# Forming a layer's new h in the block of the projection that it adds, with other steps for the sums behind it

## The chip, the cores and the metric

The kernel runs on one core of one Trainium2 chip. The metric is the device time of one execution in microseconds (us), the median over runs. The engines are named as the profile names them: PE is TensorE (matmuls; PEld its weight loads), ACT is ScalarE, DVE is VectorE, POOL is GpSimd, SP is SyncE, which here issues most transfers.

## The reference, cut to what matters

Two layers over a sequence of 512 positions with 2048 channels. Layer 0 is an attention and recurrent block, layer 1 a gated block with mixing along the sequence. After each, a gate product adds a projection of a second input:

```python
for i in range(2):
    xn = rms_norm(h, norm_pre[i])
    ...                                     # layer 0: y from attention and recurrence
    proj = xn @ c_w_in[j]                   # layer 1: 2048 x 6144
    u, v, g = _split(proj, (2048, 2048, 2048))
    oc = chunked_spatial_gating(u, v, ...)  # u * (tril(w_s) @ layer_norm(gelu(v)) + b_s), 16 groups
    y = (oc * jax.nn.silu(g)) @ c_w_out[j]
    h = h + rms_norm(y, norm_post[i])
    h = h + (p[i] @ ple_w_proj[i]) * jax.nn.sigmoid(h @ ple_w_gate[i])
```

The diff lies in three places: the last line of layer 0 (the gate product), the scaling by `norm_pre[1]` that opens layer 1, and the mixing in `chunked_spatial_gating`.

## The kernel before, in words

All operands are float32, split in a high and a low part, so that a product needs three matmuls: high by high, low by high, high by low. A big product is made by `seven`, a scheme of seven products in place of eight over blocks of the operands. Sums and differences of blocks are its operands; `sums` makes them (`x2`, `s1`, `s24`, `s3`, `x22`), and `put` and `finish` write each as a high part (a cast on ACT, L973) and a low part (a subtraction on DVE, L974) into its place. Places are slots with names: `yl0` to `yl15`, `xl0` to `xl15`, `yh0` to `yh15`, `xh0` to `xh3`; with `SETS`, the operand of `x2` goes into yl0 to yl7 and that of `s24` into xl0 to xl15.

Each product walks over its weights in eight pieces, a pair of column blocks over 14 products in 112 pieces. Each piece is cast on ACT (`whi`, L1544) and its low part made on DVE (`wlo`, L1545); every fifth piece goes to a place of its own, `half0` and `half1`. Four places for `whi` and `wlo` and one for `half` let the two engines be five pieces ahead of PE. At every piece `tick` counts one up and runs the side steps that are due; `later(n, step)` puts a step n pieces ahead. A scheduler then places each instruction in its engine's queue by priority and its own costs; each engine works its queue in order.

`first_gate` makes layer 0's gate product. The projection's blocks `pj[q, e]` come back from DRAM (`qd`, L1115) into slots whose old operands are no longer needed: (4,0), (5,0), (0,0), (1,0) into `xh0`; (2,0), (3,0) into yl0, yl1; (2,1), (3,1), (0,1), (1,1) into yl2 to yl5; (6,0), (7,0) into yl6, yl7; (6,1), (7,1), (4,1), (5,1) into xl0 to xl3. When a block of the product is done, `emit` runs: sigmoid on ACT (L1155), times `pj` on DVE (L1156), added to `H[q, e]` in its place (L1157), squared on ACT (L1159), squares summed on DVE (L1161). A save of 256 KB, `hd<-yh`, is issued on SP (L1163; every H block has a yh slot). Sixteen pieces later `scaled` multiplies H in its place by `norm_pre` on ACT, in two halves (L1169, 32 in all). It writes what the save reads, so it waits until that save has landed. `issue_after` keeps it behind the weight cast of its piece.

The sums of layer 1 take the scaled H: `early` and `x2` during the last pieces of the gate product, the others as steps in the first pieces of the next stage. In `layer_c` (values V, then U and G) the function `mix` does one of 16 groups of the mixing: it loads values and weights, normalizes (L1668 on ACT), splits into high and low part (L1678 to L1684) and multiplies with three matmuls (L1689 to L1691), at −11, −4, 0 and 5 pieces around its place.

Of the kernel before, what the change touches and what calls it, by code (L numbers as in the profile page):

```python
# [11 lines left out]
AF = mybir.ActivationFunctionType  # L12
ALU = mybir.AluOpType
# [56 lines left out]
def f(ap):  # L70
    return ap.bitcast(F32)
# [35 lines left out]
class Net:  # L107
# [986 lines left out]
    def first_gate(self, H, state, wp, ps):  # L1094
        nc, tc, i = self.nc, self.tc, self.i
        s, update, s1, s24, s3, x22 = state
        npre = self.cols["norm_pre"]
        accq, seen, pj, last = [], [False, False], {}, {}

        def places():  # L1100
            accq.extend((self.t(wp, [P, T], "accq", bufs=1), self.rstdB))

        def late(q):
            update(q, 1)
            update(q + 4, 1)
            s1(q)

        def first(q):
            with tc.high_priority(150):
                s24(q)  # L1110

        def fetch(tiles, *which):
            for (q, e), tl in zip(which, tiles):
                pj[q, e] = tl.rearrange("p (a t) -> p a t", a=2)
                nc.sync.dma_start(pj[q, e], self.qd[:, 2 * q : 2 * q + 2, e * 256 : e * 256 + 256])  # L1115

        def first_fetch():
            tl = self.t(self.xp, [P, 4, T], "xh0")
            fetch([tl[:, k, :] for k in range(4)], (4, 0), (5, 0), (0, 0), (1, 0))

        def next_fetch(n, *which):
            fetch([self.slot("yl", n + k, F32) for k in range(len(which))], *which)

        def x4():
            s[4] = self.place(("xh", (0, 3)))

        def x7():
            s[7] = self.place(("xh", (1, 2)))

        C = self.sums(H, wp, SETS)  # L1130
        cs, x2 = C[0], C[2]

        def early(q):
            if q == 0:
                cs[1] = self.whole_set()
            self.put(cs[1], q, H[q, 0])

        steps = [((1, 6, 19, 28)[q], lambda q=q: late(q)) for q in range(4)]
        steps += [((11, 15, 32, 35)[q], lambda q=q: first(q)) for q in range(4)]
        steps += [((23, 26, 43, 45)[q], lambda q=q: s3(q)) for q in range(4)]  # L1140
        steps += [(17, first_fetch), (22, places), (21, x7)]
        steps += [(34, lambda: next_fetch(0, (2, 0), (3, 0))), (44, lambda: next_fetch(2, (2, 1), (3, 1), (0, 1), (1, 1)))]
        steps += [(49, x4)]
        steps += [(50 + q, lambda q=q: x22(q)) for q in range(4)]
        steps += [(76, lambda: next_fetch(6, (6, 0), (7, 0)))]
        steps += [(90, lambda: fetch([self.slot("xl", k, F32) for k in range(4)], (6, 1), (7, 1), (4, 1), (5, 1)))]
        steps += [(103 + q, lambda q=q: early(q)) for q in range(4)]
        steps += [(110 + 2 * q, lambda q=q: x2(q)) for q in range(4)]
        for n, step in sorted(steps, key=lambda x: x[0]):
            self.later(n, step)  # L1150

        def emit(pr, m, n, src):
            e, q = m // 2, 2 * n + m % 2
            sv = src.rearrange("p (a t) -> p a t", a=2)
            last["act"] = nc.scalar.activation(src, src, AF.Sigmoid)  # L1155
            nc.vector.tensor_tensor(sv, sv, pj[q, e], ALU.mult)  # L1156
            nc.vector.tensor_tensor(H[q, e], H[q, e], sv, ALU.add)  # L1157
            sq = self.tmp(wp, "sq") if seen[e] else accq[e].rearrange("p (a t) -> p a t", a=2)
            nc.scalar.activation(sq, H[q, e], AF.Square)  # L1159
            if seen[e]:  # L1160
                nc.vector.tensor_tensor(accq[e], accq[e], sq.rearrange("p a t -> p (a t)"), ALU.add)  # L1161
            seen[e] = True
            nc.sync.dma_start(self.hd[:, 2 * q : 2 * q + 2, e * 256 : e * 256 + 256], H[q, e])  # L1163

            def scaled():
                for a in range(2):
                    c = 16 + 2 * q + a
                    with tc.issue_after(self.cast.ins):
                        nc.scalar.activation(H[q, e][:, a, :], H[q, e][:, a, :], AF.Copy, scale=npre[:, c : c + 1])  # L1169

            self.later(16, scaled)

        W = i["ple_w_gate"][0]
        self.seven(FIRST(*[Pair(W, 2 * j * T, 2 * j, emit) for j in range(2)]), Sets(s), ps, fm=True)
        s1, s24, s3, x22 = C[3:]
        steps = [(17 + 2 * q, lambda q=q: s1(q)) for q in range(4)]
        steps += [(25 + 3 * q, lambda q=q: s24(q)) for q in range(4)]
        steps += [(37 + 3 * q, lambda q=q: x22(q, True)) for q in range(4)]
        steps += [(48 + 3 * q, lambda q=q: s3(q)) for q in range(4)]
        return accq, last["act"], cs, steps  # L1180

# [434 lines left out]
    def layer_c(self, cp, sets, steps, accq, after, wp, ps):  # L1616
        nc, tc, i = self.nc, self.tc, self.i
# [29 lines left out]
        def mix(g, at):  # L1647


            gs = slice(g * P, (g + 1) * P)  # L1650
            fl = lambda x: x.rearrange("p m c -> p (m c)")
            own = {}

            def load():
                par = self.t(wp, [P, T], "accq", bufs=1) if g % 2 else self.rstdB
                own["ws"], own["bc"] = par[:, 0:P], par[:, P : 3 * P].rearrange("p (a c) -> p a c", c=P)
                vn = own["vn"] = self.t(wp, [P, 4, P], "sq")
                with tc.issue_after(self.cast.ins):
                    nc.scalar.dma_start(vn, self.vd[:, g])
                nc.scalar.dma_start(own["ws"], i["c_w_s"][0, g])  # L1660
                nc.scalar.dma_start(own["bc"][:, 0, :], i["c_ln_g"][0, gs].partition_broadcast(P))
                nc.scalar.dma_start(own["bc"][:, 1, :], i["c_ln_b"][0, gs].partition_broadcast(P))

            def norm():
                ws, bc, vn = own["ws"], own["bc"], own["vn"]
                row = lambda j: bc[:, j : j + 1, :].broadcast_to([P, 4, P])
                for m in range(4):
                    nc.scalar.activation(  # L1668
                        vn[:, m, :], vn[:, m, :], AF.Identity, bias=nb[:, m : m + 1], scale=rv[:, m : m + 1]
                    )  # L1670
                nc.gpsimd.affine_select(ws, ws, [[-1, P]], ALU.is_ge, 0.0, 0, 1)
                nc.vector.tensor_tensor(vn, vn, row(0), ALU.mult)
                nc.vector.tensor_tensor(vn, vn, row(1), ALU.add)

            def split():
                vn = own["vn"]
                pw = self.t(ps, [P, P], "mm")
                nc.tensor.transpose(pw, own["ws"], self.ident)  # L1678
                w2 = own["w2"] = self.t(lp, [P, 2, P], "w2", F32R)
                nc.scalar.copy(w2[:, 0], pw)  # L1680
                nc.vector.tensor_tensor(w2[:, 1], pw, f(w2[:, 0]), ALU.subtract)
                vh, vl = own["v"] = [self.t(wp, [P, 4, P], "sg", F32R) for _ in range(2)]
                nc.scalar.copy(vh, vn)
                nc.vector.tensor_tensor(vl, vn, f(vh), ALU.subtract)  # L1684

            def mul():
                w2, (vh, vl) = own["w2"], own["v"]
                pm = self.t(ps, [P, 4, P], "mm")
                nc.tensor.matmul(fl(pm), w2[:, 0], fl(vh), start=True, stop=False)  # L1689
                nc.tensor.matmul(fl(pm), w2[:, 0], fl(vl), start=False, stop=False)  # L1690
                nc.tensor.matmul(fl(pm), w2[:, 1], fl(vh), start=False, stop=True)  # L1691
                ub = u[g // 4][:, :, g % 4 * P : g % 4 * P + P]
                nc.vector.scalar_tensor_tensor(ub, pm, self.bsT[:, g : g + 1], ub, ALU.add, ALU.mult)

            for n, step in ((-11, load), (-4, norm), (0, split), (5, mul)):
                self.later(at + n, step)

        V = [Pair(W, D + 2 * j * T, 2 * j, vals) for j in range(2)]
# [36 lines left out]
        def done(step):  # L1735
# [28 lines left out]
            for j in range(2):  # L1764
                if step == nv + 14 * j + 1:
                    for e in range(8):
                        mix(8 * j + e, 40 + int(6.8 * e))
# [281 lines left out]
```

## Time and profile before

| | us |
|---|---|
| runs (3), median | 2232.8 |
| lowest, highest | 2230.08, 2234.23 |
| profiled execution | 2231.2 |
| its span | 2229.5 |
| PE busy | 2191.7 (98%) |
| DVE busy | 1660.8 (74%) |
| ACT busy | 1355.4 (61%) |

The span is the time that the profiler sees between the first and the last instruction; 1.7 us lie around it. Times of rows are us from the span's start. PE's busy time at the lower granted clock counts as busy, so its share does not show that loss; the column PEclk of the table by stretches does. The gate product of layer 0 fills 1230 to 1376, layer 1's product with c_w_in follows, with mixing from about 1610 to 1860.

### The profile page before, as it was taken

To read this page: it belongs to the slowest core of one execution; us is meant where nothing else is said; L and a number is where in the kernel's file an instruction comes from. 1 tells how busy PE (TensorE), PEld (TensorE's weight loads), DVE (VectorE), ACT (ScalarE), POOL (GpSimd) and SP (SyncE) were. 2 spreads that over 40 slices of the span, in tenths; PEclk is the share of its full clock that TensorE was granted. 3 is DMA by queue.
4 is the path that set the end of the run, shared out by engine and by line. 5 is a ranking of instruction groups with operands and counts; after the bars stand their busy time and mean duration, and the time that the engine had idled before them with its cause. 6 is when DMAs were issued, how large, how long until landed. Compare 5 with 4: busy or idle time off the path is not lost. (4 is left out here: it accounts for less than half of the span.)

```text
span 2229.5 us, 43456 instructions
## 1 busy us (share of the span) xinstructions
PE 2191.7 (98%) x16535; PEld 1876.3 (84%) x16535; DVE 1660.8 (74%) x3228; ACT 1355.4 (61%) x2764; POOL 311.6 (14%) x360
## 2 busy tenths in 40 slices
PE   9999999999999999999999999999999999999998
PEld 7878888888888788889999998787877878999887
DVE  8766667656734777886879877886677678978977
ACT  5545545555544677775667656755566567757754
POOL 2001010101000000000210121311121221120031
PEclk9999999999999999999999999999999999999999
DMA  7322322223233633327897887788779777688796
GB/s 237 93 78 62 84 77 79 72 64 89 69 99 95 207 103 101 97 84 208 169 226 231 201 204 190 178 211 222 167 160 231 170 187 185 146 192 271 208 242 169
DMA packets 304143, 343.34 MB, mean 154 GB/s; under 512 B 15757, under 2 KB 187950, under 8 KB 302910
## 3 DMA queue, kind: packets, MB, share of 16 engines
q1 hardware_dynamic: 237438, 240.93, 34.7%
q0 software_dynamic: 44608, 85.99, 22.5%
q10 hardware_dynamic: 21888, 13.64, 2.2%
q8 instruction: 130, 2.13, 0.4%
q14 instruction: 79, 0.65, 0.1%
HBM read 305.61 MB, written 34.90 MB: 153 GB/s over the span
## 5 line engine op out<-in xcount | busy, mean ns | idle before, releaser
L1545 DVE TENSOR_TENSOR wlo<-rq,whi 128x512 fp32r<-128x512 f32 x485 | 330.6, 688 | 138.4 <-ACT whi L1544 135.3
L1544 ACT CAST whi<-rq 128x512 fp32r<-128x512 f32 x485 | 298.4, 621 | 189.5 <-PE mm L1580 121.4
L213 PE MATMUL mm<-xh,whi 128*128 128x512 f32 x992 | 411.7, 415 | 0.0
L215 PE MATMUL mm<-xh,wlo 128*128 128x512 f32 x992 | 391.8, 395 | 0.0
L214 PE MATMUL mm<-xl,whi 128*128 128x512 f32 x992 | 389.6, 393 | 0.0
L197 ACT CAST whi<-raw 128x512 fp32r<-128x512 f32 x272 | 168.0, 619 | 149.9 <-PE mm L214 103.2
L199 DVE TENSOR_TENSOR wlo<-raw,whi 128x512 fp32r<-128x512 f32 x272 | 186.0, 695 | 92.6 <-ACT whi L197 70.0
L215 PEld LDWEIGHTS mm<-xh,wlo 128*128 128x128 f32 x992 | 186.2, 188 | 41.2
L213 PEld LDWEIGHTS mm<-xh,whi 128*128 128x128 f32 x992 | 186.9, 188 | 33.2
L214 PEld LDWEIGHTS mm<-xl,whi 128*128 128x128 f32 x992 | 187.1, 189 | 29.8
L1580 PE MATMUL mm<-whi,yh 128*128 128x512 f32 x424 | 138.2, 394 | 1.6 <-ACT whi L1544 1.6
L1580 PE MATMUL mm<-whi,yl 128*128 128x512 f32 x420 | 138.6, 395 | 0.6 <-ACT comb L1591 0.6
L1580 PE MATMUL mm<-whi,xl 128*128 128x512 f32 x424 | 137.9, 392 | 0.4 <-DVE xl L974 0.4
L1545 DVE TENSOR_TENSOR wlo<-raw,whi 128x512 fp32r<-128x512 f32 x154 | 105.0, 688 | 43.6 <-ACT whi L1544 43.3
L1544 ACT CAST whi<-raw 128x512 fp32r<-128x512 f32 x154 | 94.3, 620 | 59.0 <-PE mm L1580 40.7
L1580 PE MATMUL mm<-xh,whi 128*128 128x256 f32 x696 | 126.9, 283 | 0.0
L1580 PEld LDWEIGHTS mm<-xh,whi 128*128 128x128 f32 x696 | 108.7, 192 | 0.1
L1580 PE MATMUL mm<-xl,whi 128*128 128x256 f32 x520 | 99.5, 291 | 7.3 <-ACT whi L1544 4.4
L1545 DVE TENSOR_TENSOR half<-rq,half 128x512 fp32r<-128x512 f32 x111 | 76.4, 688 | 34.2 <-ACT half L1544 34.1
L1492 POOL DMA_DIRECT2D rq<-in_c_w_in_dram x56 | 67.6, 1220 | 242.3 <-DVE wlo L1545 162.2
L1580 PE MATMUL mm<-xh,wlo 128*128 128x256 f32 x348 | 98.5, 283 | 0.0
L1544 ACT CAST half<-rq 128x512 fp32r<-128x512 f32 x111 | 69.0, 621 | 45.9 <-PE mm L1580 27.7
(525 smaller groups left out, 5191.0 us busy)
## 6 DMA issues: line engine op xcount, KB each, us to landing
raw<-in_ab_w_in_dram SPq DMA_DIRECT2D x128, 512.0 KB, 3.9
rq<-in_c_w_in_dram POOLq DMA_DIRECT2D x56, 512.0 KB, 7.8
rq<-in_c_w_in_dram SPq DMA_DIRECT2D x50, 512.0 KB, 3.8
rq<-in_ple_w_gate_dram SPq DMA_DIRECT2D x44, 512.0 KB, 7.1
rq<-in_ple_w_gate_dram POOLq DMA_DIRECT2D x36, 512.0 KB, 9.1
raw<-in_c_w_in_dram SPq DMA_DIRECT2D x26, 512.0 KB, 6.8
rq<-in_c_w_out_dram SPq DMA_DIRECT2D x24, 512.0 KB, 5.2
rq<-in_ab_w_out_dram POOLq DMA_DIRECT2D x20, 512.0 KB, 8.1
```

Source lines behind the costliest of these rows:

```text
L197: nc.scalar.copy(hi[:, : m * n], src)
L199: self.weng.tensor_tensor(lo[:, : m * n], src, f(hi[:, : m * n]), ALU.subtract)
L213: nc.tensor.matmul(acc, hi, xhi[k], start=(k == 0), stop=False)
L214: nc.tensor.matmul(acc, hi, xlo[k], start=False, stop=False)
L215: nc.tensor.matmul(acc, lo, xhi[k], start=False, stop=(k == nk - 1))
L1492: nc.gpsimd.dma_start(view(tl), block(*where), accum_op=ALU.add)
L1544: self.cast = nc.scalar.copy(hi, src)
L1545: nc.vector.tensor_tensor(lo, src, f(hi), ALU.subtract)
L1580: nc.tensor.matmul(o, x, y, start=(first and r == 0 and j == 0 and not a), stop=(r == 7 and j == 2), **more)
```

## The change

`emit` adds into `pj[q, e]`'s place instead of `H[q, e]`; square and save read it there. `scaled` reads it there as well, writes H, comes three pieces later instead of sixteen, and is not tied to a weight cast. The four `x2` come at 108 to 111 instead of 110 to 116. In the next stage s1 begins at 8 instead of 17, s24 at 17 (every fourth piece) instead of 25 (every third), x22 at 35 instead of 37. `mul` of the mixing comes at 7 instead of 5.

```diff
--- before.py
+++ after.py
@@ -1145,7 +1145,7 @@
         steps += [(76, lambda: next_fetch(6, (6, 0), (7, 0)))]
         steps += [(90, lambda: fetch([self.slot("xl", k, F32) for k in range(4)], (6, 1), (7, 1), (4, 1), (5, 1)))]
         steps += [(103 + q, lambda q=q: early(q)) for q in range(4)]
-        steps += [(110 + 2 * q, lambda q=q: x2(q)) for q in range(4)]
+        steps += [(108 + q, lambda q=q: x2(q)) for q in range(4)]
         for n, step in sorted(steps, key=lambda x: x[0]):
             self.later(n, step)
 
@@ -1154,28 +1154,28 @@
             sv = src.rearrange("p (a t) -> p a t", a=2)
             last["act"] = nc.scalar.activation(src, src, AF.Sigmoid)
             nc.vector.tensor_tensor(sv, sv, pj[q, e], ALU.mult)
-            nc.vector.tensor_tensor(H[q, e], H[q, e], sv, ALU.add)
+            o = pj[q, e]
+            nc.vector.tensor_tensor(o, H[q, e], sv, ALU.add)
             sq = self.tmp(wp, "sq") if seen[e] else accq[e].rearrange("p (a t) -> p a t", a=2)
-            nc.scalar.activation(sq, H[q, e], AF.Square)
+            nc.scalar.activation(sq, o, AF.Square)
             if seen[e]:
                 nc.vector.tensor_tensor(accq[e], accq[e], sq.rearrange("p a t -> p (a t)"), ALU.add)
             seen[e] = True
-            nc.sync.dma_start(self.hd[:, 2 * q : 2 * q + 2, e * 256 : e * 256 + 256], H[q, e])
+            nc.sync.dma_start(self.hd[:, 2 * q : 2 * q + 2, e * 256 : e * 256 + 256], o)
 
             def scaled():
                 for a in range(2):
                     c = 16 + 2 * q + a
-                    with tc.issue_after(self.cast.ins):
-                        nc.scalar.activation(H[q, e][:, a, :], H[q, e][:, a, :], AF.Copy, scale=npre[:, c : c + 1])
-
-            self.later(16, scaled)
+                    nc.scalar.activation(H[q, e][:, a, :], o[:, a, :], AF.Copy, scale=npre[:, c : c + 1])
+
+            self.later(3, scaled)
 
         W = i["ple_w_gate"][0]
         self.seven(FIRST(*[Pair(W, 2 * j * T, 2 * j, emit) for j in range(2)]), Sets(s), ps, fm=True)
         s1, s24, s3, x22 = C[3:]
-        steps = [(17 + 2 * q, lambda q=q: s1(q)) for q in range(4)]
-        steps += [(25 + 3 * q, lambda q=q: s24(q)) for q in range(4)]
-        steps += [(37 + 3 * q, lambda q=q: x22(q, True)) for q in range(4)]
+        steps = [(8 + 2 * q, lambda q=q: s1(q)) for q in range(4)]
+        steps += [(17 + 4 * q, lambda q=q: s24(q)) for q in range(4)]
+        steps += [(35 + 3 * q, lambda q=q: x22(q, True)) for q in range(4)]
         steps += [(48 + 3 * q, lambda q=q: s3(q)) for q in range(4)]
         return accq, last["act"], cs, steps
 
@@ -1692,7 +1692,7 @@
                 ub = u[g // 4][:, :, g % 4 * P : g % 4 * P + P]
                 nc.vector.scalar_tensor_tensor(ub, pm, self.bsT[:, g : g + 1], ub, ALU.add, ALU.mult)
 
-            for n, step in ((-11, load), (-4, norm), (0, split), (5, mul)):
+            for n, step in ((-11, load), (-4, norm), (0, split), (7, mul)):
                 self.later(at + n, step)
 
         V = [Pair(W, D + 2 * j * T, 2 * j, vals) for j in range(2)]
```

`emit` is one line longer now, so what was L1157 to L1163 is L1158 to L1164 in the rows of the changed kernel.

**ACT, behind the blocks (0,0) and (1,0) of the gate product.** yh0 and yh2 are their H; `xh0_3094` is the four-block tile of pj; `xh0_3211` is the operand that takes its place; xl6 and xl14 are operands of the running product. Words in brackets are the semaphores waited for; DMAHW is one of SP's transfers. Before:

```order
L1544 CAST half0_3207_16212<-rq1_3078_15512 128x512 [waits PE_49,Activation_49]
L973 CAST xh0_3211_16250<-yh13_2954_14957 128x512
L1169 ACTIVATE yh0_2704_13397<-yh0_2704_13397,col89_72_254 128x256 [waits DMAHW7_49,Activation_49]
L1544 CAST whi_3209_16234<-rq2_3183_16072 128x512 [waits DMAHW1_49,PE_49]
L1169 ACTIVATE yh0_2704_13397<-yh0_2704_13397,col89_72_254 128x256
L973 CAST xl6_3165_15971<-sq_3164_15969 128x512 [waits DVE_49]
L1544 CAST whi_3213_16252<-rq2_3183_16072 128x512 [waits PE_49]
L1169 ACTIVATE yh2_2706_13403<-yh2_2706_13403,col89_72_254 128x256 [waits DMAHW0_49,Activation_49]
L973 CAST xl14_3168_15977<-sg_3167_15975 128x512 [waits DVE_49]
```

Now:

```order
L1169 ACTIVATE yh0_2704_13397<-xh0_3094_15569,col89_72_254 128x256
L1160 ACTIVATE sq_3152_15911<-xh0_3094_15569 128x512 [waits DVE_49]
L1544 CAST half0_3207_16216<-rq1_3078_15512 128x512 [waits PE_49,Activation_49]
L1169 ACTIVATE yh0_2704_13397<-xh0_3094_15569,col89_72_254 128x256
L1169 ACTIVATE yh2_2706_13403<-xh0_3094_15569,col89_72_254 128x256
L1544 CAST whi_3209_16234<-rq2_3183_16076 128x512 [waits DMAHW1_49,PE_49,Activation_49]
L973 CAST xl6_3165_15975<-sq_3164_15973 128x512 [waits DVE_49]
L1169 ACTIVATE yh2_2706_13403<-xh0_3094_15569,col89_72_254 128x256
L1544 CAST whi_3213_16252<-rq2_3183_16076 128x512 [waits PE_49,Activation_49]
L973 CAST xl14_3168_15981<-sg_3167_15979 128x512 [waits DVE_49]
L973 CAST xh0_3211_16250<-yh9_2958_14972 128x512 [waits DMAHW4_49,DMAHW7_49,DMAHW0_49,Activation_49]
```

L1169 waits for no transfer; the casts into `xh0` stand one behind the other and the first waits for three transfers, of which DMAHW7 and DMAHW0 are the saves of these two blocks.

**DVE, at x2(0).** yl1_3372 before and yl1_3368 now is the low part of the first block of that operand; yl1's earlier content is pj of (3,0). Before:

```order
L1545 TENSOR_TENSOR wlo_3246_16507<-rq1_3078_15512,whi_3245_16506 128x512 [waits PE_49,Activation_49]
L1157 TENSOR_TENSOR yh6_2789_13900<-yh6_2789_13900,mm_3154_15912 128x512 [waits DVE_49]
L1545 TENSOR_TENSOR wlo_3250_16526<-rq2_3183_16072,whi_3249_16525 128x512 [waits DMASW0_49,PE_49,Activation_49]
L974 TENSOR_TENSOR yl1_3372_17379<-yh8_2671_13221,yl0_3371_17378 128x512
L1161 TENSOR_TENSOR accq_3112_15682<-accq_3112_15682,sq_3228_16384 128x512 [waits Activation_49]
L1545 TENSOR_TENSOR wlo_3252_16542<-rq2_3183_16072,whi_3251_16541 128x512 [waits PE_49,Activation_49]
L1545 TENSOR_TENSOR wlo_3254_16559<-rq3_3188_16107,whi_3253_16558 128x512 [waits DMASW1_49,PE_49,Activation_49]
```

Now:

```order
L1545 TENSOR_TENSOR wlo_3246_16511<-rq1_3078_15512,whi_3245_16510 128x512 [waits PE_49,Activation_49]
L1158 TENSOR_TENSOR yl1_3160_15951<-yh6_2789_13900,mm_3154_15916 128x512 [waits DVE_49]
L1545 TENSOR_TENSOR wlo_3250_16530<-rq2_3183_16076,whi_3249_16529 128x512 [waits DMASW0_49,PE_49,Activation_49]
L1162 TENSOR_TENSOR accq_3112_15682<-accq_3112_15682,sq_3228_16384 128x512 [waits Activation_49]
L1545 TENSOR_TENSOR wlo_3252_16546<-rq2_3183_16076,whi_3251_16545 128x512 [waits PE_49,Activation_49]
L1545 TENSOR_TENSOR wlo_3254_16563<-rq3_3188_16111,whi_3253_16562 128x512 [waits DMASW1_49,PE_49,Activation_49]
L974 TENSOR_TENSOR yl1_3368_17362<-yh8_2671_13221,yl0_3367_17361 128x512 [waits DMAHW6_49,DVE_49,Activation_49]
L1545 TENSOR_TENSOR half1_3256_16579<-rq3_3188_16111,half0_3255_16578 128x512 [waits PE_49,Activation_49]
```

The row L974 now stands two weight pieces later and waits for DMAHW6, the save of (3,0); the low parts of the next pieces, the first into `half1`, are queued behind it.

**PE, at the fourth mixing (sg_3961, sg_3962 are the high and low part of its values).** Before:

```order
L1580 MATMUL mm_3975_20004<-wlo_3978_20009,xl0_3478_17819 128x512
L1580 MATMUL mm_3975_20004<-whi_3977_20008,xl1_3479_17820 128x512
L1689 MATMUL mm_3979_20018<-sg_3961_19941,w2_3960_19938 128x512
L1690 MATMUL mm_3979_20018<-sg_3962_19942,w2_3960_19938 128x512
L1691 MATMUL mm_3979_20018<-sg_3961_19941,w2_3960_19938 128x512
L1580 MATMUL mm_3974_20003<-whi_3980_20023,xl0_3478_17819 128x512
```

Now:

```order
L1580 MATMUL mm_3975_20004<-whi_3982_20031,xl2_3474_17788 128x512
L1580 MATMUL mm_3975_20004<-wlo_3983_20032,xl2_3474_17788 128x512
L1580 MATMUL mm_3975_20004<-whi_3982_20031,xl3_3475_17789 128x512
L1689 MATMUL mm_3984_20041<-sg_3961_19941,w2_3960_19938 128x512
L1690 MATMUL mm_3984_20041<-sg_3962_19942,w2_3960_19938 128x512
L1691 MATMUL mm_3984_20041<-sg_3961_19941,w2_3960_19938 128x512
L1678 MATMUL mm_3985_20046<-ident_37_114,rstdB_2579_12736 128x128
```

Two weight pieces (`whi_3979`, not shown, and `whi_3982`) have come between; the mixing's three matmuls are followed by the next group's transposition, L1678.

**DVE, at the same mixing.** Before:

```order
L1545 TENSOR_TENSOR wlo_3978_20009<-rq2_3893_19639,whi_3977_20008 128x512 [waits Activation_49]
L1496 TENSOR_TENSOR rq5_3914_19731<-rq5_3914_19731,rq1_3997_20100 128x1024 [waits DMAHW7_49,DVE_49]
L1545 TENSOR_TENSOR wlo_3981_20024<-rq2_3893_19639,whi_3980_20023 128x512 [waits Activation_49]
L1681 TENSOR_TENSOR w2_3960_19938<-mm_3959_19936,w2_3960_19938 128x128
L1545 TENSOR_TENSOR wlo_3984_20037<-rq3_3899_19673,whi_3983_20036 128x512 [waits Activation_49]
L1684 TENSOR_TENSOR sg_3962_19942<-sq_3924_19770,sg_3961_19941 128x512
```

Now:

```order
L1545 TENSOR_TENSOR wlo_3978_20009<-rq2_3893_19639,whi_3977_20008 128x512 [waits Activation_49]
L1496 TENSOR_TENSOR rq5_3913_19726<-rq5_3913_19726,rq1_3997_20100 128x1024 [waits DMAHW7_49,DVE_49]
L1545 TENSOR_TENSOR wlo_3980_20019<-rq2_3893_19639,whi_3979_20018 128x512 [waits Activation_49]
L1693 SCALAR_TENSOR_TENSOR xh2_3789_19155<-mm_3958_19931,bsT_3505_17897,xh2_3789_19155 128x4x128 [waits DVE_49]
L1681 TENSOR_TENSOR w2_3960_19938<-mm_3959_19936,w2_3960_19938 128x128
L1545 TENSOR_TENSOR wlo_3983_20032<-rq3_3899_19673,whi_3982_20031 128x512 [waits Activation_49]
L1684 TENSOR_TENSOR sg_3962_19942<-sq_3924_19770,sg_3961_19941 128x512
```

L1684, which makes the low part for the second matmul, stood behind the low parts of two pieces (`wlo_3981`, `wlo_3984`) that PE multiplies only after the mixing; now it stands right behind `wlo_3983`, the last piece that PE multiplies ahead of it.

## Rows read from the trace of the kernel before

**Rows 1.** The page, part 1: busy time, share, instructions

```profile
PE 2191.7 (98%) x16535; PEld 1876.3 (84%) x16535; DVE 1660.8 (74%) x3228; ACT 1355.4 (61%) x2764; POOL 311.6 (14%) x360
```

**Rows 2.** Timeline of PE: start, duration, instruction, [idle before <-releaser]

```profile
1269.38 0.38 PE L1580 MATMUL mm<-xl,whi 128*128 128x256 f32 x1 [2.17 <-ACT xl L973]
...
1346.37 0.80 PE L1580 MATMUL mm<-xl,whi 128*128 128x256 f32 x2 [4.11 <-ACT whi L1544]
...
1403.30 1.05 PE L1743 MATMUL mm<-ones,rstdB 128*128 128x2 f32 x8 [0.74 <-DVE rstdB L1161]
```

**Rows 3.** Table by stretches around the save's waits, its column line first

```profile
core 0: us, PE busy (x) PEld busy (x) DVE busy (x) ACT busy (x) POOL busy (x), PEclk, DMA share, GB/s
1266.90:1270.40 3.50, 0.70 (x5) 0.30 (x3) 1.96 (x4) 3.00 (x7) 0.00 (x0) 0.98 1.10 192
1270.40:1274.70 4.30, 4.30 (x24) 4.30 (x25) 3.46 (x6) 2.44 (x5) 1.33 (x2) 0.62 0.59 81
1290.00:1304.00 14.00, 14.00 (x119) 14.00 (x118) 9.52 (x15) 7.49 (x13) 4.71 (x4) 1.00 1.00 232
1326.00:1337.00 11.00, 10.76 (x90) 10.56 (x88) 7.34 (x13) 6.96 (x15) 3.42 (x3) 1.00 1.09 239
1337.00:1346.40 9.40, 3.96 (x25) 3.14 (x25) 3.24 (x6) 3.06 (x7) 1.20 (x1) 0.94 0.89 191
1346.40:1352.40 6.00, 6.00 (x27) 5.78 (x28) 3.83 (x6) 3.44 (x7) 2.41 (x2) 0.52 0.55 81
```

**Rows 4.** Timeline of ACT, same columns

```profile
1267.39 0.51 ACT L1169 ACTIVATE yh<-yh,col 128x256 f32<-128x256 f32 x1 [3.25 <-DMA hd<-yh]
...
1268.73 0.60 ACT L973 CAST xl<-sq 128x512 fp32r<-128x512 f32 x1
...
1269.76 0.51 ACT L1169 ACTIVATE yh<-yh,col 128x256 f32<-128x256 f32 x1
...
1305.45 0.51 ACT L1169 ACTIVATE yh<-yh,col 128x256 f32<-128x256 f32 x1 [1.89 <-DMA hd<-yh]
...
1335.57 0.91 ACT L1169 ACTIVATE yh<-yh,col 128x256 f32<-128x256 f32 x2 [3.84 <-DMA hd<-yh]
...
1345.30 0.51 ACT L1169 ACTIVATE yh<-yh,col 128x256 f32<-128x256 f32 x1 [4.86 <-DMA hd<-yh]
...
1400.61 0.91 ACT L1169 ACTIVATE yh<-yh,col 128x256 f32<-128x256 f32 x2 [3.48 <-DMA hd<-yh]
```

**Rows 5.** View of line L1169: what its engine stood idle for

```profile
  DMA hd<-yh: 18.8, 6
```

**Rows 6.** Timeline of SP's queue: issues of the saves, L1163

```profile
1261.01 1.67 SPq L1163 DMA_DIRECT2D hd<-yh  x2
...
1292.98 1.09 SPq L1163 DMA_DIRECT2D hd<-yh  x1
...
1326.14 1.56 SPq L1163 DMA_DIRECT2D hd<-yh  x2
...
1332.16 0.36 SPq L1163 DMA_DIRECT2D hd<-yh  x1
```

**Rows 7.** View of line L1163: issue to landing

```profile
DMA to landing us min/median/max: 3.3/4.2/5.1
```

**Rows 8.** Timeline of PE: two uses of a `half` weight piece

```profile
1294.85 1.60 PE L1580 MATMUL mm<-xh,half 128*128 128x256 f32 x12
...
1302.05 1.60 PE L1580 MATMUL mm<-xh,half 128*128 128x256 f32 x12
```

**Rows 9.** Timeline of DVE: the low part for the second of them

```profile
1297.07 0.69 DVE L1545 TENSOR_TENSOR half<-rq,half 128x512 fp32r<-128x512 f32 x1 [0.76 <-ACT half L1544]
```

**Rows 10.** Timeline of DVE at the present x2(1)

```profile
1332.65 0.69 DVE L974 TENSOR_TENSOR yl<-yh,yl 128x512 fp32r<-128x512 f32 x1
1337.02 0.69 DVE L1545 TENSOR_TENSOR wlo<-rq,whi 128x512 fp32r<-128x512 f32 x1 [3.68 <-ACT whi L1544]
```

**Rows 11.** Groups of lines, 1600 to 1860: busy us, mean ns | idle, releasers

```profile
L1668 ACT ACTIVATE sq<-sq,nb,rv 128x128 f32<-128x128 f32 x62 | 28.2, 491 | 41.4 <-DMA sq<-vd 41.4
...
L1690 PE MATMUL mm<-sg,w 128*128 128x512 f32 x15 | 6.1, 407 | 1.8 <-DVE sg L1684 1.8
```

## The prediction

> **What bounds the kernel now.** The page first: TensorE is busy for 2191.7 us of the 2229.5 us span [rows 1], so time can only come from its idle stretches, 37.8 us in all, and from stretches at the lower clock. I then listed TensorE's rows in order of time and kept those with idle time before them. Three lie where the diff works [rows 2]: 2.17 us before 1269.38, released by a cast of an operand on ScalarE (L973); 4.11 us before 1346.37, released by a weight cast; and 0.74 us before 1403.30, released by VectorE's sum of squares. The table by stretches prices the first two [rows 3]. Of 1266.9 to 1270.4, TensorE works 0.70 of 3.50 us, and for the next 4.3 us the granted clock is 0.62, a mix of the 2.4 and the 1.2 GHz level. Of 1337 to 1346.4 it works 3.96 of 9.40 us, and the 6.0 us after that are granted 0.52, nearly all of it at 1.2 GHz.
>
> Why was the cast late? ScalarE's own rows tell it [rows 4]: the scaling L1169, which overwrites h in its place, stood 3.25 us until 1267.39, 3.84 us until 1335.57 and 4.86 us until 1345.30, each time until the save `hd<-yh` of the same block had read it. The line's view adds these up: 18.8 us in 6 waits [rows 5]. ScalarE works in order, so the operand cast at 1268.73 and every weight cast behind L1169 waited too.
>
> How long does a save take? SyncE's rows give the issue [rows 6], ScalarE's release gives the end: block (3,0) issued at 1292.98, released 1305.45, so 12.5 us; (3,1) 1326.14 to 1335.57, 9.4 us; (1,1) 1332.16 to 1345.30, 13.1 us. The DMA engines are full there (share 1.00 in 1290 to 1304, 1.09 in 1326 to 1337 [rows 3]). The view of the save's line disagrees: 3.3 to 5.1 us to landing [rows 7]. The Trainium skill ("DMA: Bandwidth & Descriptors", section on the anatomy of one DMA) gives, for DMAs of GpSimd's path, 2.0 us plus the bytes over 436 GB/s; for a save of 256 KB that is an estimate of 2.6 us, and the releases took 3.6 to 5 times as long. I go by the releases, since L1169 waits for nothing but its save there; the landing view is the ground of a rival.
>
> **What the change does, part by part.** Instruction counts stay as they are; only operands and places in the queues move.
>
> 1. *L1169 no longer waits.* It reads h from pj's place and writes H, which no DMA reads; it stands directly behind the square, three ticks after the sum. The first stall goes, since the operand cast then comes at its due time: 3.50 − 0.70 = 2.80 us idle and 4.30 × (1 − 0.62) = 1.6 us of clock, 4.4 us. The second goes too: 9.40 − 3.96 = 5.4 us, 0.24 us in the stretch before (11.00 − 10.76) and 6.0 × (1 − 0.52) = 2.9 us of clock, 8.6 us [rows 3]. The 0.74 us before 1403.30 go, as the last L1169 pair there waited too (3.48 us until 1400.61 [rows 4]). Together 13.7 us.
>
> 2. *The wait moves to who next writes pj's place.* Nothing else may write there until the save has landed. The order of the changed kernel shows such waits at these places:
>  - *The cast into xh0* (ScalarE, saves of (0,0) and (1,0)). The two saves are issued from 1261.01 [rows 6], ScalarE comes to the cast near 1267, and the second save was done by 1269.76 at the latest, when its L1169 ran without a wait [rows 4]. So 0 to 3 us of waiting. TensorE takes a piece 1.44 us after the last (five pieces between the two uses of `half`, (1302.05 − 1294.85)/5 [rows 8]), and the weight buffers let the casts be five pieces, 7.2 us, ahead. Cost 0; without that cover, up to 3 us.
>  - *x2(0)*, now at steps 108 to 111. Its low part on VectorE (L974, into yl1) stands ahead of the low part of `half`, which came at 1297.07 [rows 9], and waits for save (3,0). At the measured 12.5 us that is 1305.45 in the old clock of the trace. Then L974 and the low part follow, about 0.6 us each: 1306.7. TensorE wants that `half` at 1302.05 [rows 8]: 4.6 us idle. All later low parts are queued behind it, but VectorE makes one in 0.6 us and catches up. For the clock I take 2.6 us, between the 1.6 us that followed 2.8 idle and the 2.9 that followed 5.4 [rows 3]. Cost 7.2 us. Below: 0, if the save lands in the 5.1 us of rows 7 (1298.1, and 1299.3 is before 1302.05). Above: about 8, with the 13.1 us of the slowest save. I take the middle row because it is this very save, in the same traffic; that the work runs 4.4 us earlier shifts issue, loads and need alike.
>  - *x2(1)*: its L974 (into yl3) waits for (3,1), released at 1335.57 [rows 4]. VectorE reaches it near 1333.3 and waits about 2.3 us, where it has so far idled 3.68 us before 1337.02 anyway [rows 10]. The five pieces of lead cover it.
>  - *x2(2) and x2(3)*: the place of (1,1) is wanted near 1349 and was free at 1345.30, if its save is issued as late as before; (6,0) and (7,0) are issued late, at 1357 to 1360, with the loads of the next layer. Waits of 0 to 6 us against 7.2 us of lead. I put 1.0 us for x2(1) to x2(3) together; below 0, above 5.
>
> 3. *The sums' other steps* (s1, s24, x22 of the next stage). The same casts and sums come some 2 to 9 ticks earlier on two engines that are not the bound there. The places that s24 fills come free with saves issued well before. Taken as nothing; VectorE's slack hides it, and a cast pushed by one such pair would come about 0.7 us later.
>
> 4. *The mixing's matmuls two ticks later.* Of the 15 recorded starts of L1690, TensorE waited 1.8 us for the split's low part (L1684) [rows 11], nearly all in mixes 3 and 11, where that part stood right ahead of its use. Two more weight pieces, some 2.7 us, now stand between. That removes 1.8 us. Against it: only two places for the splits and one for the weights, so the next split and the load behind it sit closer to their use. ScalarE already waits 41.4 us for the values [rows 11], hidden by the same lead. I keep 1.0 us of the 1.8; bounds −3 (three more such late splits of 0.9, as in these two mixes) to 1.8 us.
>
> The sum: −13.7 + 7.2 + 1.0 − 1.0 = −6.5 us, from the profiled execution's 2231.2 us to 2224.7. That execution lies 1.6 us under the median of the runs, 2232.8; a forecast between the two bases is **2225 us**.
>
> **The rivals.**
> - *The saves land in time.* If L974 in x2(0) does not outlast the lead, items 1 and 4 remain whole: −13.7 − 1.0 + 0 to 1 = about −14.5, so 2217. For it: the landing view [rows 7], and DMA traffic that may be ordered otherwise. Against it: the wait that ended at 1305.45. By the Trainium skill's 2.6 us this would be the outcome; none of the three releases bears that figure out.
> - *Only an exchange.* Stalls like that of x2(0) at two of the four x2 places: −14.7 + 2 × 7.2 = −0.3, so 2231. It needs one further save as slow as (1,1), whose place x2(2) wants about 4 us after its old release. For it: with L1169 out of the way, ScalarE and VectorE reach the later x2 up to 4 us sooner against the saves than they did.
> - *Slower: VectorE stalls behind saves at three or four places.* The mechanism: its L974 stands in the in-order queue ahead of the low parts. It decides from the point where a save lands over 7.2 us after VectorE reaches the row, and in x2(0) that wait is 9 us. Three places: −14.7 + 3 × 7.2 = +6.9, so 2238. For it: steps 108 to 111 bring all four x2 one to five ticks nearer to their saves. Against it: in x2(1) the measured release leaves 2.3 us of wait, and DMA share falls to 0.55 after 1346.4 [rows 3]. The Trainium skill ("TensorE: Matmul & The Clock Gate", architectural detail) speaks against the change here: VectorE and ScalarE are strict first-in, first-out, so one waiting row holds all behind it. The trace agrees: the cast at 1268.73 had nothing to wait for but the row ahead.
> - *It does not do what it says*: the scheduler might have put L1169 back behind a wait. The order rows exclude it for the scaling itself.
>
> **How the numbers follow.** One stall, at x2(0): 0.43, 2225 (its own range 2221 to 2228). No stall: 0.27, 2217. Exchange: 0.18, 2231. Slower: 0.12, 2238. The range for 8 in 10 reaches from 2215, 2 us under the no-stall case, to 2236, which leaves out most of the slower case. About 0.2% (4.5 us) is what a measurement here can tell from nothing: faster than 2228 are the first two cases, 0.70; the exchange is the same, 0.18; slower 0.12.
>
> **What would show it.** In the changed profile L1169 has no idle time released by `hd`, TensorE has no idle row near 1265 and none of 4 us near 1337, and no stretch at half clock there. VectorE's L974 near 1292 (the old 1296 less 4.4) waits about 9 us for a save, with TensorE idle 4 to 5 us and some 5 us at half clock behind it: if that row has no wait, the first rival is right. Waits of the same kind at the next three x2 that TensorE feels would show the exchange or the slower case. L1690 loses its 1.8 us of idle time. The sum would be wrong if a stall appears at no place named here, in the loads above all.

## The result, and the profile after

| | before | changed |
|---|---|---|
| median of 13 runs each, us | 2231.4 | 2226.42 |
| ratio, 95% interval | | 0.9976 (0.9967 to 0.9985) |
| profiled execution, us | 2231.2 | 2223.7 |
| its span, us | 2229.5 | 2222.0 |

The change makes the kernel 0.24% faster, about 5 us. One run of each kernel was far slower (3030.85 and 5371.09 us) and stands outside the ratio, though it is counted in the medians. In the two profiled executions the difference is 7.5 us. I began with the page's first part for the changed kernel:

```profile
PE 2185.6 (98%) x16535; PEld 1872.1 (84%) x16535; DVE 1659.4 (75%) x3228; ACT 1353.2 (61%) x2764; POOL 301.9 (14%) x360
```

TensorE has 36.4 us without work left, 1.4 less than before. The rest of the 7.5 us is busy time, 6.1 us less than in [rows 1], most of it time that ran at the lower clock. Then the table by stretches, over the places of [rows 3] (the columns are those of its first line):

```profile
1262.00:1270.00 8.00, 8.00 (x69) 8.00 (x69) 7.61 (x13) 6.40 (x13) 3.62 (x3) 1.00 1.09 220
1290.00:1302.20 12.20, 8.93 (x75) 8.72 (x73) 3.54 (x7) 5.76 (x11) 3.42 (x3) 1.00 1.02 226
1302.20:1308.00 5.80, 5.77 (x48) 5.77 (x49) 5.25 (x8) 1.93 (x4) 0.00 (x0) 1.00 1.09 279
1326.00:1345.00 19.00, 19.00 (x161) 19.00 (x160) 14.79 (x26) 13.03 (x26) 6.05 (x5) 1.00 1.10 241
```

The first and the last line are the two old stalls: TensorE works through both at full clock. The second line holds a new one. TensorE's and VectorE's timelines name it, and TensorE's shows one more row that matters, in the mixing:

```profile
1302.23 1.46 PE L1580 MATMUL mm<-xh,half 128*128 128x256 f32 x10 [3.30 <-DVE half L1545]
...
1672.65 0.77 PE L1580 MATMUL mm<-whi,yh 128*128 128x512 f32 x1 [3.22 <-ACT whi L1544]
```

```profile
1292.17 0.69 DVE L1545 TENSOR_TENSOR wlo<-rq,whi 128x512 fp32r<-128x512 f32 x1 [0.54 <-ACT whi L1544]
1300.88 0.69 DVE L974 TENSOR_TENSOR yl<-yh,yl 128x512 fp32r<-128x512 f32 x1 [8.02 <-DMA hd<-yl]
1301.49 0.68 DVE L1545 TENSOR_TENSOR half<-rq,half 128x512 fp32r<-128x512 f32 x1
```

VectorE stood 8.02 us at x2(0) for the save of (3,0) and made the low part of `half` right after it; TensorE went on 0.74 us after that row's start. The view of L1169 lists no transfer any more; the view of L974 now has what stood there in [rows 5]:

```profile
  DMA hd<-yl: 14.3, 3
```

The other two of its three waits are 2.72 us at x2(1) and 3.57 us at x2(3). TensorE feels neither. ScalarE still waits for saves at two casts, into xh0 and at x2(3), as the view of the save's line (L1164) says; TensorE does not feel these either:

```profile
  ACT yl L973: 2.3, 1
  ACT xh L973: 1.4, 1
```

Last, the mixing, in the groups of lines:

```profile
L1668 ACT ACTIVATE sq<-sq,nb,rv 128x128 f32<-128x128 f32 x64 | 28.4, 487 | 49.6 <-DMA sq<-vd 49.6
...
L1690 PE MATMUL mm<-sg,w 128*128 128x512 f32 x16 | 6.3, 393 | 0.0
```

The 1.8 us before L1690 are gone [rows 11]. But ScalarE now waits 49.6 us for the values to be mixed (43.6 before, over all 64 rows of the line), and behind it weight casts come late, as in the row of TensorE at 1672.65. ScalarE's row just before that, and the table by stretches just after it:

```profile
1670.83 0.49 ACT L1668 ACTIVATE sq<-sq,nb,rv 128x128 f32<-128x128 f32 x1 [6.81 <-DMA sq<-vd]
```

```profile
1672.70:1676.10 3.40, 3.40 (x7) 2.37 (x8) 3.40 (x7) 3.40 (x8) 0.28 (x1) 0.50 0.55 145
```

Summed over TensorE's rows, the idle time of the mixing went from 5.5 to 9.3 us, and the stretch at half clock costs 1.7 us more. The kernel before has no lower clock in its mixing.

### The profile page after: what moved, and what is told of

Same layout as the page of the kernel before. It is cut to its first block, busy times and chain, and to the rows that moved or that the text cites. A ratio compares the mean times of both kernels' runs of the same rounds, so it can differ in the third digit from the quotient of the medians.

```text
span 2222.0 us, 43469 instructions
## 1 busy us (share of the span) xinstructions
PE 2185.6 (98%) x16535; PEld 1872.1 (84%) x16535; DVE 1659.4 (75%) x3228; ACT 1353.2 (61%) x2764; POOL 301.9 (14%) x360
## 4 chain that ended last, share of the span: by engine, by line
PE 79%; DVE 8%; DMA 6%; ACT 4%; issue 2%; ACTq 0%; DVEq 0%; SPq 0%; POOLq 0%
PE mm L1580 37%; PE mm L213 10%; PE mm L215 9%; PE mm L214 9%; DMA sq<-vd 3%; DVE wlo L1545 2%; PE tm L551 1%; DMA rq<-in_ple_w_gate_dram 1%; PE tm L572 1%; ACT whi L1544 1%; PE g L923 1%; PE pp L340 1%; PE tm L484 1%; PE tm L910 1%; PE ch L636 1%
## 5 line engine op out<-in xcount | busy, mean ns | idle before, releaser
L1544 ACT CAST whi<-rq 128x512 fp32r<-128x512 f32 x485 | 297.4, 620 | 186.3 <-PE mm L1580 120.1
L1544 ACT CAST whi<-raw 128x512 fp32r<-128x512 f32 x154 | 94.9, 620 | 69.0 <-PE mm L1580 48.5
L1580 PEld LDWEIGHTS mm<-whi,yh 128*128 128x128 f32 x424 | 80.3, 189 | 23.3 <-ACT whi L1544 6.8
L1544 ACT CAST half<-rq 128x512 fp32r<-128x512 f32 x111 | 68.8, 620 | 46.0 <-PE mm L1580 26.9
```

Source lines behind the costliest of these rows:

```text
L1544: self.cast = nc.scalar.copy(hi, src)
L1580: nc.tensor.matmul(o, x, y, start=(first and r == 0 and j == 0 and not a), stop=(r == 7 and j == 2), **more)
```

## The experiments

All times are medians; each ratio, with its 95% interval, is to the kernel before on the same chip. E1 to E4 share one set of runs of the kernel before (median 2232.01 us), E5 to E8 another (2229.96 us). Lines in these kernels are shifted by four from E3 on, so that L1544, L1668 and L1690 become L1548, L1672 and L1694.

**E1, the mixing's matmuls back at 5 pieces, the rest as changed.**

```diff
-            for n, step in ((-11, load), (-4, norm), (0, split), (7, mul)):
+            for n, step in ((-11, load), (-4, norm), (0, split), (5, mul)):
```

> The changed kernel with the mixing's matmuls back at 5 pieces; all else as changed. Theory A (the two pieces cost what the mixing lost: TensorE's idle time between 1590 and 1860 went from 5.5 us before to 9.3 after, because the split's places come free later, the values are loaded later and ScalarE waits longer for them at L1668): the idle time of the mixing falls back to about 5.5 us with the 0.9 us rows at L1690 there again, ScalarE's wait for the values from 49.6 to about 43.6 us, and the time is 3 to 4 us under the changed kernel, near 2219 in the profiled run. Rival B (the mixing lost by the other phase of its loads, since everything comes 9 us earlier): idle stays near 9 us and the time stays within 1 us of the changed kernel.

2220.76 us, ratio 0.9955 (0.9940 to 0.9970), against 0.9976 for the whole change. ScalarE's wait for the values is 45.4 us, TensorE's idle time in the mixing 6.1 us, and two rows of 0.93 and 0.79 us at L1690 are back. Theory A's direction, and a little more than its size: 0.21% is 4.7 us, to which the two intervals leave some 4 us on either side.

The profiled execution, 2223.92 us, is no shorter than that of the changed kernel (2223.7), where theory A put it near 2219: it paid more at x2(0), whose queues are the same. So it shows the price of that stall in full. Timeline of TensorE, then the table by stretches behind it:

```profile
1302.88 2.50 PE L1580 MATMUL mm<-xh,half 128*128 128x256 f32 x10 [4.33 <-DVE half L1545]
```

```profile
1302.80:1306.00 3.20, 3.12 (x14) 3.12 (x15) 2.58 (x6) 0.62 (x1) 0.00 (x0) 0.50 1.12 213
1306.00:1312.00 6.00, 6.00 (x42) 6.00 (x41) 3.35 (x5) 1.86 (x3) 0.00 (x0) 0.77 0.75 273
```

Here 4.33 us of idling were followed by 3.2 us at 1.2 GHz and 6.0 us at 0.77, some 3.0 us of clock. In the changed kernel's own profile 3.30 us of idling were followed by full clock.

**E2, the kernel before with the matmuls at 7 pieces, nothing else.** The edit is that of the change, in the old kernel.

> The kernel before with the mixing's matmuls at 7 pieces, nothing else. Theory A (the two pieces alone cost it): TensorE's idle time in the mixing rises from 5.5 to about 9 us, the time by 3 to 4 us over the kernel before (ratio 1.0015 to 1.002). Rival B: idle stays near 5.5 or falls by the 1.8 us of L1690, the time is that of the kernel before or 1.8 us under it (ratio 0.999 to 1.0).

2237.16 us, ratio 1.0026 (1.0013 to 1.0039). Slower by some 5.8 us, more than the 3 to 4 of theory A; idle time of the mixing 9.2 us, ScalarE's wait 48.4 us, no idle time at L1690. Theory A's direction again, so the cost belongs to this one number and not to the earlier arrival of everything. The profile alone would not show it: between 1225 and 1380, where the queues are those of the kernel before, it idles 11.1 us against 8.75.

**E3, x2 behind its weight casts, the rest as changed.** The step numbers turned out to move nothing: with 110 + 2q in place of 108 + q the order of ScalarE's queue is the same row for row, probably since the scheduler takes these casts as soon as their operands exist. What moves them is a tie to the weight cast of a piece:

```diff
+        def x2_behind(q):
+            with tc.issue_after(self.cast.ins):
+                x2(q)
+
-        steps += [(108 + q, lambda q=q: x2(q)) for q in range(4)]
+        steps += [((74, 94, 109, 111)[q], lambda q=q: x2_behind(q)) for q in range(4)]
```

> The changed kernel with the casts of x2 queued behind the weight casts of pieces 74, 94, 109 and 111; the step numbers alone move nothing in the queues. Theory A (L974 of x2(0) stood 8.0 us for the save in front of the half, and TensorE 3.3 us for that half): with L974 eight weight pieces later the save has landed, L974 shows no wait over 1 us, the 3.30 us row of TensorE near 1302 is gone, 3 to 3.5 us under the changed kernel plus whatever clock its other runs lose there. Rival B (the DMA queue is the bound there, so that a wait for weights takes the place of the stall): TensorE idles 2 us or more elsewhere between 1290 and 1370, released by a transfer, and the time is within 1 us of the changed kernel.

2219.49 us, ratio 0.9947 (0.9931 to 0.9963). VectorE's timeline at x2(0), where L974 stands seven weight pieces later in its queue (not eight, as expected):

```profile
1299.26 0.69 DVE L1549 TENSOR_TENSOR wlo<-raw,whi 128x512 fp32r<-128x512 f32 x1 [0.75 <-ACT whi L1548]
1299.87 0.68 DVE L974 TENSOR_TENSOR yl<-yh,yl 128x512 fp32r<-128x512 f32 x1
```

L974 runs without a wait, though the save's last part had landed only 0.4 us before. TensorE idles 0.27 us in all between 1225 and 1380, and the view of L974 lists no transfer. From 0.9976 to 0.9947 is 0.29%, 6.5 us, with some 4 us on either side. Of it 3.3 us is the idling; that the rest is clock lost there in other executions fits E1, but is not shown run by run. The edit moves all four x2, not x2(0) alone. Theory A; of rival B's transfer nothing is seen.

**E4, both edits.**

> Both edits together: x2 behind its weight casts and the mixing's matmuls at 5 pieces. If both costs stand by themselves: 6.5 to 7.5 us under the changed kernel, profiled near 2216, ratio to the kernel before near 0.994. If one of the two only passes its gain on: no better than the better one of the two alone, about 2219 to 2220.

2215.6 us, ratio 0.9929 (0.9913 to 0.9945), 3.9 us under E3 and 5.2 us under E1 on the same chip. By the ratios it is 10.5 us under the changed kernel, more than expected, and the two costs add up within the error. Its profiled execution (2218.93 us) is the slowest of its six runs; TensorE idles 10.6 us in its mixing and runs some 3 us of it at half clock, so that single profiles of the mixing differ by more than the edits do, and I go by the medians.

**E7, of the change only the new place of h is left: E4 with the next stage's sums at the old steps.**

```diff
-        steps = [(8 + 2 * q, lambda q=q: s1(q)) for q in range(4)]
-        steps += [(17 + 4 * q, lambda q=q: s24(q)) for q in range(4)]
-        steps += [(35 + 3 * q, lambda q=q: x22(q, True)) for q in range(4)]
+        steps = [(17 + 2 * q, lambda q=q: s1(q)) for q in range(4)]
+        steps += [(25 + 3 * q, lambda q=q: s24(q)) for q in range(4)]
+        steps += [(37 + 3 * q, lambda q=q: x22(q, True)) for q in range(4)]
```

> x2 behind its casts, matmuls at 5 pieces, and the next stage's sums at the old steps: of the change only the new place of h is left. Theory A (the sums' steps are worth nothing, they lie in the slack of ScalarE and VectorE): the time of the kernel with the new steps, 2215.6, within 1.5 us. Rival B (they carry part of the gain, since the scaled h comes earlier and the sums were late): 2 us or more slower, with TensorE's idle rows between 1380 and 1450 larger than 1.0 us in all.

2212.43 us, ratio 0.9925 (0.9911 to 0.9939), E4's 0.9929 within the error; TensorE idles 1.3 us between 1380 and 1450, 1.0 in E4. In the profiles the same stretch of TensorE's matmuls (those from 1380 to 1575 in the kernel before) takes 190.5 us in E4 and 190.8 in E7. So theory A: the sums' steps are worth nothing that can be measured. The times alone would leave room for 4 us; the stretches do not.

**E8, the matmuls at 9 pieces, x2 as in E3.**

```diff
-            for n, step in ((-11, load), (-4, norm), (0, split), (7, mul)):
+            for n, step in ((-11, load), (-4, norm), (0, split), (9, mul)):
```

> x2 behind its casts, the mixing's matmuls at 9 pieces: the suspected cost once more. Theory A (each piece that the matmuls move back holds the split's places longer): slower than at 7 pieces (2219.5) by a similar step as from 5 to 7, 2 to 5 us, near 2223, with ScalarE's wait for the values above 48 us. Rival B (the step from 5 to 7 was a matter of which row stands where, not of the places held): within 1.5 us of 2219.5 on either side.

2212.23 us, ratio 0.9924 (0.9909 to 0.9939): faster than with 7 (0.9947), the same as with 5 (0.9925 in E7). The step from E3 is 5 us, just clear of its error. ScalarE's wait for the values is 42.4 us, the least of the kernels so far. So theory A of this run is refuted: it is not that each piece costs. Rival B's number, within 1.5 us of 2219.5, is missed too. What E8 has in common with 5 pieces is the shorter wait.

**E5, the scaling of the loaded values later in ScalarE's queue; matmuls at 7 pieces, x2 as in E3.**

```diff
                 for m in range(4):
-                    nc.scalar.activation(
-                        vn[:, m, :], vn[:, m, :], AF.Identity, bias=nb[:, m : m + 1], scale=rv[:, m : m + 1]
-                    )
+                    with tc.issue_after(self.cast.ins):
+                        nc.scalar.activation(
+                            vn[:, m, :], vn[:, m, :], AF.Identity, bias=nb[:, m : m + 1], scale=rv[:, m : m + 1]
+                        )
...
-            for n, step in ((-11, load), (-4, norm), (0, split), (7, mul)):
+            for n, step in ((-11, load), (-2, norm), (0, split), (7, mul)):
```

> x2 behind its weight casts, the mixing's matmuls at 7 pieces as in the change, and the scaling of the loaded values (the four activations on ScalarE) queued behind the weight cast of two pieces ahead of the split, so that 3 to 9 weight casts instead of 2 or 3 stand between the issue of a load of values and its use. Theory A (ScalarE's wait for these loads, longer with the later places of the split, is what the two pieces cost): ScalarE's wait for the values falls from 48 to under 15 us, TensorE's idle time in the mixing from 8 or 9 to under 5 us, and the time is 3 to 5 us under the same kernel without this edit (2219.5), near 2215. Rival B (the loads are not the bound; the split's own parts or DVE's queue are): ScalarE's wait falls, TensorE's idle time stays, and the time is within 1.5 us of 2219.5.

2202.82 us, ratio 0.9879 (0.9862 to 0.9896), 15 us under E3 by the ratios. Theory A, and three times the gain that I gave it. Groups of lines of the mixing's stretch for E3, then for E5 (its L1673 is E3's L1672), with a product of TensorE:

```profile
L1672 ACT ACTIVATE sq<-sq,nb,rv 128x128 f32<-128x128 f32 x64 | 28.4, 487 | 48.2 <-DMA sq<-vd 48.1
...
L1584 PE MATMUL mm<-wlo,xl 128*128 128x512 f32 x82 | 32.9, 401 | 0.4 <-DVE wlo L1549 0.2
L1584 PE MATMUL mm<-wlo,yl 128*128 128x512 f32 x78 | 31.1, 398 | 1.8 <-DVE wlo L1549 1.6
```

```profile
L1673 ACT ACTIVATE sq<-sq,nb,rv 128x128 f32<-128x128 f32 x64 | 28.7, 488 | 6.6 <-DMA sq<-vd 6.5
...
L1584 PE MATMUL mm<-wlo,xl 128*128 128x512 f32 x87 | 33.9, 389 | 0.0
L1584 PE MATMUL mm<-wlo,yl 128*128 128x512 f32 x78 | 30.4, 389 | 0.0
```

The wait falls from 48.1 to 6.5 us and TensorE's idle time in the mixing from 8.05 to 0.22 us. The mean of these products falls from about 400 to 389 ns, but that does not make each one shorter: the median of TensorE's 128x512 products is 389 ns in both. E3 has 54 of 1232 that took over 450 ns, eight of them over 550 ns in a stretch at half clock from 1654.2 on; E5 has 24 over 450 ns and no lower clock there.

Idle time is not all of the gain. Counted from start to start, the same 1346 matmuls (those from 1575 to 1880 in the kernel before) take 310.2 us in E3 and 294.0 in E5. Of these 16.2 us, 8 are idle time and, by estimate, 1.7 the half clock; the others are delays that the profile counts as busy, since these products are drawn 389 ns long and start some 218 ns apart, so that a short delay opens no gap. Over the whole span TensorE is busy for 2177.3 us against 2182.9; the two spans, 2215.1 and 2202.5, differ by 12.6 us, as E5's profile was slower ahead of layer 0's gate product.

**E6, the same with the matmuls at 5 pieces and the scaling at −4.**

> The same with the matmuls at 5 pieces and the scaling behind the cast of four pieces ahead (3 to 7 casts between load and use). Theory A: little is left to gain there, as the loads cost less at 5 pieces: 0 to 3 us under the kernel with x2 behind and matmuls at 5 (2215.6), the two rows of 0.9 us at L1694 remain. Rival B: no change against 2215.6. If the two rows of L1694 decide, this is slower than the kernel with 7 pieces by 1.7 us.

2202.09 us, ratio 0.9878 (0.9862 to 0.9895): the fastest kernel here, 1.2% under the kernel before, and the same as E5. Theory A was right that the wait decides, and wrong that little was left at 5 pieces: 46.4 us of waiting in E4 are 5.8 us here, and the time is 0.5% less, 11 us where it allowed 3. The rows of 0.9 us at L1694 are gone as well; TensorE's timeline shows no idle time between 1575 and 1900. With the wait gone, 5 and 7 pieces take the same time.

## Why the prediction came out, step by step

The total was right: 2225 us forecast, 2226.42 measured, inside the range and the likeliest case's own (2221 to 2228). Of its five terms, three were right in kind and size, one in kind, and one had the wrong sign.

*L1169 no longer waits, −13.7 us.* Right, perhaps a little small. E7 has this part alone, with x2(0) out of the way: 0.75% under the kernel before, 16.7 us, and its interval reaches from 13.6 to 19.8. In the two first profiles the same matmuls around the three places take 4.8, 9.7 and 0.8 us less, 15.3 in sum. Both stalls of [rows 2] are gone, the half clock behind them too, and the 0.74 us before 1403.30.

*The cast into xh0, 0.* Right: ScalarE waited 1.4 us there, within the 0 to 3 that I gave it, and TensorE felt nothing.

*x2(0), +7.2 us.* Right. The wait was 8.0 us where I said 9, the idle time 3.3 us in one profile and 4.33 in another where I said 4.6, and the clock behind it cost 0 in the one and 3.0 us in the other where I said 2.6. By the medians its whole price is 5.2 to 6.5 us (E1 to E4, and the change to E3). The save landed 11.2 us after its issue at 1289.67, by the release; the landing view of the changed kernel says 4.0 to 5.1 us, and my estimate by the Trainium skill's fit ("DMA: Bandwidth & Descriptors", anatomy of one DMA) was 2.6. I was wrong that this view disagrees with the releases [rows 7]: in either profile it could time only two of the 16 saves, (2,0) among them with 5.1 us, and none that L1169 or L974 waited for. So it gave no ground for the rival of saves that land in time, which fell with the wait. As to why the save took long, the Trainium skill ("DMA: Bandwidth & Descriptors", section on queues, rings and completion order) says that each DMA engine takes its descriptors in ring order and turns between the queues that have work. That fits a save that stands among full queues (DMA share 1.02 in the stretch before 1302.2), though no run here took the other transfers away.

*x2(1) to x2(3), +1.0 us.* In the changed kernel's profile two waits, of 2.7 and 3.6 us on VectorE; TensorE felt nothing: 0. In E1, whose queues are the same there, x2(1) waited 5.16 us and TensorE 0.94 us behind it. So the lead of five pieces covers these waits nearly, but not always.

*The sums' steps, 0.* Right (E7). What I did not see: the new steps for x2 don't move it at all. I read the order of the changed kernel as the work of those steps; it is the scheduler's, and the same with the old steps.

*The mixing, −1.0 us.* Here a step failed, though the total did not show it: "I keep 1.0 us of the 1.8; bounds −3 (three more such late splits of 0.9, as in these two mixes) to 1.8 us". The 1.8 us at L1690 went as forecast, but the change at this place costs about 4 to 6 us in sum (E1 against the change 4.7, E4 against E3 3.9, E2 against before 5.8). The bound was taken from the wrong row. I priced late splits, and the price lay in the row that I called hidden: the 41.4 us that ScalarE waits for the values [rows 11]. Those waits use up the five pieces of lead, and what goes beyond reaches TensorE, as in ScalarE's row at 1670.83 above. By wait and ratio, with h and x2 as in E3, the sums new in all but E7:

| kernel | ScalarE's wait for the values, us | ratio to before | the 1346 matmuls of the mixing in its profile, us |
|---|---|---|---|
| E3, 7 pieces | 48.1 | 0.9947 | 310.2 |
| E4, 5 pieces | 46.4 | 0.9929 | 313.2 |
| E7, 5 pieces, old sums | 44.1 | 0.9925 | 306.3 |
| E8, 9 pieces | 42.4 | 0.9924 | 303.9 |
| E5, 7 pieces, scaling later | 6.5 | 0.9879 | 294.0 |
| E6, 5 pieces, scaling later | 5.8 | 0.9878 | 293.7 |

The order of wait and ratio is the same, though the times tell only three levels apart: E3; E4, E7 and E8; E5 and E6. The last column is one execution of each kernel (305.0 us in the kernel before, 310.7 in the changed one), and E4's was the slowest of its six. Part of the price is clock: the profiles of the changed kernel, E2, E3 and E4 each have a stretch at half clock in the mixing, of about 1.7 us, behind an idle row of 1.5 to 3.2 us; the others have none. I had no term for that.

That 5 and 7 pieces take the same time once the wait is gone (E5 and E6) shows that the number of pieces costs nothing by itself. How it lengthens the wait is read from the queue and not shown by a run: two weight casts lie between the load of a group's values and their scaling in most groups; with 5 pieces it is three in mixes 3, 6, 7 (counted from 0) and their like in the second half, with 7 it is two there. With 9 pieces it is two as well, though, and yet the wait is shorter: why those loads land sooner was not settled.

The parts from the medians: −16.7 (E7), +6 for x2(0), +4.7 for the mixing is −6.0 us; measured −5.4 by the ratio. Each part is uncertain by 3 to 4 us. By these figures the total of −6.5 us owes its closeness to luck in part: a cost missed by 5.7 us in the mixing met a gain taken 3 us too small, with the rest made up by x2(0) to x2(3).

## What to carry to other kernels

When a wait is removed by letting a result lie in another buffer, look for who writes that buffer next, and in which queue that row stands: here 18.8 us of waiting left ScalarE and 14.3 us came back on VectorE and 3.7 on ScalarE; in the changed kernel's profile TensorE felt one long wait where it had felt two. A wait on an engine with slack is not free if weight casts are queued behind it; take the sum of those waits as the first thing to price, not as hidden. A step number in a scheduled kernel may do nothing: read the order, and tie a row to another one where its place matters.

## What the hardware showed beside

An idle stretch of the same length was followed by the lower clock in one execution and not in another: 2.17 and 0.63 us of idling before 1270.4 by a granted clock of 0.62 [rows 3], and in E2, whose queues are the same there, 2.19 and 0.63 us by full clock, as the second line shows (table by stretches, columns as in [rows 3]); after 8.01 us of idling the same execution ran at 0.50. Nor does the length sort them: 3.30 us at x2(0) were followed by full clock in the changed kernel's profile, and 1.49 us before 1652.4 in E3 by 0.50 from 1654.2 on.

```profile
1269.00:1272.90 3.90, 1.08 (x8) 0.68 (x6) 2.00 (x4) 2.66 (x6) 0.00 (x0) 1.00 1.09 192
1272.90:1277.00 4.10, 4.10 (x34) 4.10 (x35) 3.69 (x7) 3.39 (x7) 1.50 (x2) 1.00 0.57 79
...
1348.70:1352.00 3.30, 3.30 (x14) 3.07 (x15) 3.08 (x5) 2.67 (x6) 2.03 (x2) 0.50 0.16 13
```

So in these traces the clock's price of one short stall differs from one execution to the next. That fits the spread of the runs: those of the changed kernel lie between 2220.8 and 2230.3 us at mean granted clocks of 0.995 to 0.998, E3's between 2216.8 and 2221.4 at 0.998 to 1.000. How much of the spread is clock was not shown.
